# A two-layer hybrid attention trunk on one core: lanes are offered a turn once per row block outside the differential heads

## The chip, the cores and the metric

One core of a Trainium2 chip runs one program that computes both layers. The metric is the device time of one execution in microseconds (us). Every time below comes from such executions, or from one that a hardware profiler recorded.

## The reference

All is float32: 512 tokens of width 2048, 2 layers. Each layer normalises its input, projects it to 5952 columns, runs three groups of attention heads on slices of that, gates and concatenates them, projects back and adds a normalised residual:

```python
h = rms_norm(x, pre_w)
proj = h @ w_in                                   # 2048 x 5952
a_q, a_k, a_v, a_g, b_q, b_k, b_v, b_g, c_q, c_kv, c_kr, c_g = split(proj)
y_a = diff_attention(...)            # 4 heads, two softmaxes each, causal
y_b = sliding_window_attention(...)  # 16 query heads on 2 key heads, window 128, sinks
qc  = rms_norm(c_q, q_norm_w) @ w_uq
kvc = rms_norm(c_kv, kv_norm_w) @ w_ukv
y_c = causal_attention(...)          # 4 latent heads with a shared rotary key
y = concatenate([y_a, y_b, y_c]) * silu(concatenate([a_g, b_g, c_g]))
out = y @ w_out                                   # 2048 x 2048
return x + rms_norm(out, post_w)
```

## The kernel before

**Products in three parts.** A float32 product is made of three matmuls on a shorter format: both factors are split into a high and a low half, and high x high, high x low and low x high are summed in PSUM (`three`, line 299; each matmul is issued on line 142). The high half of a weight tile, `whi`, is a cast on ScalarE (L151), the low half, `wlo`, a subtraction of two SBUF tiles (L152) on VectorE or GpSimd. Before the line `ahead[0] = True` (L701) and from the second half of the output projection on, every other `wlo` is made on VectorE; in between all are made on GpSimd, ahead of other work.

**Row blocks.** The weights come in row blocks of 128 rows. `stream` loads two at a time on SP's queue into one of three buffers (`raw`) and yields their halves. `sweep` (L306) takes a block, or a group of two at the start and at the end of a projection, and for each bank of PSUM (a "job": one 128-token tile, or 128 columns of the result) issues its matmuls. A projection has 4 banks, or 2 where it covers half of the tokens, so a block is 12 (or 6) matmuls, and a group of two 24 (or 12). All four banks (`g`) come from one pool of four: the next projection's first bank must first have been read out by VectorE or ScalarE.

**Lanes.** The work on heads runs beside the projections as two "lanes". A lane is a Python generator whose steps issue a few TensorE instructions and the VectorE and ScalarE work that follows them, then yield a delay. `Lanes.step` runs a lane's next step only if the planner's clock, which `mm` and `transpose` advance by an assumed cost, has passed that delay (2.6 us for a split, 3.0 for a row of scores, more elsewhere, L1040 to L1053). `Lanes.tick` (L92) offers both lanes one step. `sweep` calls it after each job and after the group. `lanes.finish` forces named tasks to their end where the next part needs them. TensorE's order is the order in which Python issues it; the other engines' order is found by a scheduler.

**The order of a layer** (times of layer 0 in the profile; layer 1 repeats it):

- Feed (start; and the turn from one layer to the next): `feed` (L510) transposes 128-token tiles (`hT`), scales them (`h`) and splits them into `act_hi` and `act_lo`; at the turn `finish` (L968) first makes the residual, `ob` (L982), in whose rows the next layer's input lies. `scale` squares the same rows for the norm. Beside them run the keys' and the first queries' projections of each half of the tokens; `rotate_q` turns the queries on VectorE (L242 to L252: `q_rot`). `layer_constants` computes lambda with an Exp on ScalarE (`lam_d`, L494).
- 116 to 280 us: two gate projections, then the second queries' projection. `spread_r` makes the row scales, `sw_pair` (L652) runs two sliding-window heads: `stack_q` transposes four tiles of `q_rot` (`qT`) and splits them (`qe`, `qo`, L380 and L381), then scores (`sc`), probabilities (`p`), their transposes and split (`pT`, `pTh`, `pTl`), and the sum over values (`oT`).
- 280 to 490 us: the low-rank projections (`C_Q`, `C_KV`) with the other four pairs of heads; `latent_scale` with `rsqrt` (L160 to L165, `rsq_u`, `rlat`); the rotary queries (`qr`) and their stacks (`rotary_q`, L777); `up_kv` (L789), which needs these and the spread scale `R` before it can read out its banks (`kf`, `vl`); the gate of the latent heads, with two of them as lanes (`mla_head`).
- 498 to 725 us: the differential heads' four projections and their gate, with `da_head` as lanes.
- From 725 us: the output projection in four chunks of 512 columns, the last two in two halves of the tokens.

The loop that the change touches, and what calls it:

Of the kernel before, what the change touches and what calls it, by code (L numbers as in the profile page):

```python
# [108 lines left out]
def trunk(ctx: ExitStack, tc: tile.TileContext, ins, inv_freq, out):  # L109
# [164 lines left out]
            V.tensor_tensor(dst[:, mm_, :], src[:, mm_, :], rb, op=ALU.mult)  # L274


    ahead, behind = [False], [True]

    def stream(w, segs, nk, C, rows=0, before=None):

# [25 lines left out]
    def sweep(tiles, nk, jobs, after=None):  # L306

        def run(group):  # L310
            for job in jobs:
                for n, t in group:
                    job(t, n == 0, n == nk - 1)
                if job is not jobs[-1]:
                    lanes.tick()
            for n, t in group:
                if after:
                    after(n)
            lanes.tick()

        held = []
        for n, t in enumerate(tiles):
            held.append((n, t))
            if n in (0, nk - 2):
                continue
            run(held)
            held = []
# [219 lines left out]
    def norm_rows(name, l, tag):  # L547

        rows = []
        for n in range(4):  # L550
            rows.append(slot(name, tag))
            nc.gpsimd.dma_start(out=rows[n], in_=ins[name][l, n * S:(n + 1) * S].partition_broadcast(P))
        return rows

    def layer(l, pre, norms, r_in, start=None):
# [292 lines left out]
        for k in range(4, 12):  # L848
            gates[k] = slot("yb", "gy")
            nc.gpsimd.dma_start(out=gates[k], in_=y_spill[l][:, k - 4, :])  # L850
        stage = [0] * 5
        heads_out = [None] * 4

        def da_head(lane, h, raw, vv):
# [95 lines left out]
        done = [0]  # L950


        final = l + 1 == DEPTH
        post = norm_rows("post_norm_w", l, "k")
        nxt = None if final else column("pre_norm_w", l + 1, KT)
# [73 lines left out]
    for _ in range(N_LOAD):  # L1029
        load()  # L1030
    state = layer(0, pre, norms, r_in, start)
    for l in range(1, DEPTH):
        state = layer(l, *state)
# [41 lines left out]
```

## Time and profile before

| | |
|---|---|
| three executions | 1810.54, 1814.18 (median) and 1814.90 us |
| the profiled execution | 1823.35 us, of which the span of the trace is 1821.6 us |
| TensorE busy in the span | 1746.5 us (96%), 8832 matmuls |
| TensorE's mean granted clock | 0.986 of 2.4 GHz |
| VectorE, ScalarE, GpSimd busy | 914.7, 820.4 and 788.0 us (50, 45 and 43%) |
| DMA | 202.26 MB, 111 GB/s on the mean |

Busy time of TensorE is the union of its matmuls' times, so what is missing to the span is the time in which it waited. An instruction that waits blocks the ones behind it on its engine. A matmul of 512 columns is shown with some 0.40 us, but the next starts 0.23 us after it. The granted clock has two levels, 2.4 and 1.2 GHz; a share between is a mean over the stretch. TensorE, VectorE and ScalarE are told apart in rows as PE, DVE and ACT; POOL is GpSimd.

### The profile page before, as it was taken

What the parts mean: (1) busy time and instruction counts of PE and PEld (TensorE: products, weight loads), DVE (VectorE), ACT (ScalarE), POOL (GpSimd) and SP (SyncE); (2) the same over time, 40 slices, a digit from 0 to 9 for tenths busy, and PEclk for the clock granted to TensorE, in tenths of its full rate; (3) what the DMA queues carried; (4) which work ended last, traced back from release to release, by engine and by line L of the source; (5) the groups of instructions that cost most, each with busy time, mean ns of one, the idle gap of its engine ahead of it and who ended that gap; (6) DMA issues with size and microseconds to landing.
All of it is one profiled execution on the core that took longest, in us unless ns stands there. A gap on an engine that the chain in (4) does not pass through costs nothing. (4 is left out here: it accounts for less than half of the span.)

```text
span 1821.6 us, 25325 instructions
## 1 busy us (share of the span) xinstructions
PE 1746.5 (96%) x8832; PEld 1495.5 (82%) x8832; DVE 914.7 (50%) x2230; ACT 820.4 (45%) x1792; POOL 788.0 (43%) x666
## 2 busy tenths in 40 slices
PE   6899999999999999999979999999999999999996
PEld 5778888878899998788768788788889999888875
DVE  7754616734336658301785554275434357680033
ACT  6444524625344445325555553264444344552343
POOL 4343343343434344448334334334434434444662
PEclk9999999999999999999999999999999999999999
DMA  6542332232323233325755323322323322332366
GB/s 186 142 139 76 92 97 67 88 84 79 101 85 85 67 90 120 116 93 184 240 174 168 93 81 94 92 70 87 87 70 116 81 70 71 115 128 93 123 200 197
DMA packets 168672, 202.26 MB, mean 111 GB/s; under 512 B 30800, under 2 KB 92256, under 8 KB 168544
## 3 DMA queue, kind: packets, MB, share of 16 engines
q1 hardware_dynamic: 162160, 190.12, 35.3%
q0 software_dynamic: 3264, 10.51, 1.6%
q8 instruction: 69, 1.13, 0.3%
q10 hardware_dynamic: 3120, 0.01, 0.1%
q14 instruction: 59, 0.48, 0.1%
HBM read 188.02 MB, written 12.58 MB: 110 GB/s over the span
## 5 line engine op out<-in xcount | busy, mean ns | idle before, releaser
L152 POOL TENSOR_TENSOR wlo<-raw,whi 128x512 fp32r<-128x512 f32 (+2 forms) x608 | 758.2, 1254 | 987.9 <-ACT whi L151 955.3
L151 ACT CAST whi<-raw 128x512 fp32r<-128x512 f32 (+3 forms) x704 | 405.0, 582 | 602.8 <-PE g L142 487.7
L142 PE MATMUL g<-wlo,act_hi 128*128 128x512 f32 (+2 forms) x1408 | 523.5, 372 | 25.6 <-DVE wlo L152 23.8
L142 PE MATMUL g<-whi,act_hi 128*128 128x512 f32 (+2 forms) x1408 | 527.1, 374 | 7.2 <-ACT whi L151 7.2
L142 PE MATMUL g<-whi,act_lo 128*128 128x512 f32 (+2 forms) x1408 | 519.6, 369 | 0.0
L142 PEld LDWEIGHTS g<-wlo,act_hi 128*128 128x128 f32 x1408 | 267.9, 190 | 69.8 <-DVE wlo L152 31.7
L142 PE MATMUL g<-act_hi,whi 128*128 128x512 f32 x768 | 314.4, 409 | 0.0
L142 PE MATMUL g<-act_hi,wlo 128*128 128x512 f32 x768 | 305.9, 398 | 0.0
L142 PE MATMUL g<-act_lo,whi 128*128 128x512 f32 x768 | 305.7, 398 | 0.0
L142 PEld LDWEIGHTS g<-whi,act_hi 128*128 128x128 f32 x1408 | 268.0, 190 | 43.2 <-ACT whi L151 8.8
L142 PEld LDWEIGHTS g<-whi,act_lo 128*128 128x128 f32 x1408 | 267.8, 190 | 34.4
L142 PEld LDWEIGHTS g<-act_hi,wlo 128*128 128x128 f32 x768 | 145.6, 190 | 35.1
L142 PEld LDWEIGHTS g<-act_hi,whi 128*128 128x128 f32 x768 | 146.5, 191 | 28.6
L142 PEld LDWEIGHTS g<-act_lo,whi 128*128 128x128 f32 x768 | 146.3, 190 | 28.8
L152 DVE TENSOR_TENSOR wlo<-raw,whi 128x512 fp32r<-128x512 f32 (+1 forms) x96 | 71.3, 745 | 100.9 <-ACT whi L151 100.9
L966 DVE TENSOR_TENSOR ob<-g,post_norm_w 128x512 f32<-128x512 f32 x32 | 22.1, 691 | 192.0 <-ACT sq L964 191.9
L152 DVE TENSOR_TENSOR pTl<-pT,pTh 128x512 fp32r<-128x512 f32 (+2 forms) x112 | 67.8, 610 | 68.7 <-ACT pTh L151 68.5
L151 ACT CAST pTh<-pT 128x512 fp32r<-128x512 f32 (+2 forms) x112 | 58.6, 526 | 71.3 <-PE pT L146 70.7
L367 DVE TENSOR_TENSOR gate<-g,r_rows 128x512 f32<-128x512 f32 x32 | 22.0, 689 | 86.9 <-PE g L142 85.8
L146 PE MATMUL pT<-ident,p 128*128 128x128 f32 x384 | 61.0, 274 | 1.3 <-DVE p L833 1.3
L644 ACT ACTIVATE p<-p,nm 128x256 f32<-128x256 f32 (+1 forms) x128 | 59.8, 469 | 0.0
L438 ACT ACTIVATE p<-p,nm 128x128 f32<-128x128 f32 (+3 forms) x64 | 36.0, 562 | 49.8 <-DVE nm L437 49.8
(236 smaller groups left out, 2079.5 us busy)
## 6 DMA issues: line engine op xcount, KB each, us to landing
raw<-w_in SPq DMA_DIRECT2D x144, 512.0 KB, 3.7
raw<-w_out SPq DMA_DIRECT2D x96, 512.0 KB, 3.8
raw<-w_in SPq DMA_DIRECT2D x192, 128.0 KB, 2.4
raw<-w_in SPq DMA_DIRECT2D x32, 256.0 KB, 3.1
x<-x SPq DMA_DIRECT2D x16, 256.0 KB, 4.7
y_spill<-gate POOLq DMA_DIRECT2D x16, 256.0 KB, 2.3
raw<-w_ukv SPq DMA_DIRECT2D x8, 512.0 KB, 3.8
yb<-y_spill POOLq DMA_DIRECT2D x16, 256.0 KB, 4.1
```

The costliest lines, as they stand in the source:

```text
L142: nc.tensor.matmul(out_, a, b, start=start, stop=stop, skip_group_check=True)
L146: nc.tensor.transpose(out_, in_, ident)
L151: late(A.copy(hi, src), behind)
L152: E.tensor_tensor(lo, src, hi.bitcast(F32), op=ALU.subtract)
L367: V.tensor_tensor(gate, ps, rows, op=ALU.mult)
L438: A.activation(p, p, AF.Exp, bias=nm, scale=scale, accum_out=den)
L644: A.activation(blocks[i], blocks[i], AF.Exp, bias=nm[:, i:i + 1], scale=64.0 ** -0.5, accum_out=den[:, i:i + 1])
L966: V.tensor_tensor(ob[n][m], t, post[n], op=ALU.mult)
```

## The change

A switch, `fine`, is added. It is false at first, is set just before the differential heads' projections of a layer, and is cleared after their gate projection, ahead of the output projection. The turn after each job but the last is offered only while it is set. The turn after each group stays everywhere.

```diff
-    ahead, behind = [False], [True]
+    ahead, behind, fine = [False], [True], [False]
...
             for job in jobs:
                 for n, t in group:
                     job(t, n == 0, n == nk - 1)
-                if job is not jobs[-1]:
+                if fine[0] and job is not jobs[-1]:
                     lanes.tick()
...
         stage = [0] * 5
+        fine[0] = True
         heads_out = [None] * 4
...
         done = [0]
 
 
+        fine[0] = False
         final = l + 1 == DEPTH
```

On TensorE, at the start of layer 0's first gate projection, before (`g_1278` and `g_1279` are its first and second bank, `whi_1284` and `whi_1288` its first two row blocks):

```order
L142 MATMUL g_1278<-act_hi_88,whi_1284 128x512
L142 MATMUL g_1278<-act_lo_89,whi_1284 128x512
L142 MATMUL g_1278<-act_hi_88,wlo_1285 128x512
L142 MATMUL g_1278<-act_hi_88,whi_1288 128x512
L142 MATMUL g_1278<-act_lo_89,whi_1288 128x512
L142 MATMUL g_1278<-act_hi_88,wlo_1289 128x512
L146 MATMUL qT_1307<-ident_83,q_rot_850 128x128
L146 MATMUL qT_1307<-ident_83,q_rot_856 128x128
L146 MATMUL qT_1307<-ident_83,q_rot_1264 128x128
L146 MATMUL qT_1307<-ident_83,q_rot_1270 128x128
L142 MATMUL g_1279<-act_hi_88,whi_1284 128x512
```

and now, where `g_1281` is the fourth bank (the second and third, twelve matmuls, stand ahead of these rows):

```order
L142 MATMUL g_1281<-act_hi_88,whi_1284 128x512
L142 MATMUL g_1281<-act_lo_89,whi_1284 128x512
L142 MATMUL g_1281<-act_hi_88,wlo_1285 128x512
L142 MATMUL g_1281<-act_hi_88,whi_1288 128x512
L142 MATMUL g_1281<-act_lo_89,whi_1288 128x512
L142 MATMUL g_1281<-act_hi_88,wlo_1289 128x512
L146 MATMUL qT_1325<-ident_83,q_rot_850 128x128
L146 MATMUL qT_1325<-ident_83,q_rot_856 128x128
L146 MATMUL qT_1325<-ident_83,q_rot_1264 128x128
L146 MATMUL qT_1325<-ident_83,q_rot_1270 128x128
L142 MATMUL g_1278<-act_hi_88,whi_1338 128x512
```

The four transposes of the first query stack stood behind the first bank's six matmuls and stand now behind the fourth bank's, 18 matmuls later. The first stacks of the second four pairs, in the projection `C_Q`, move in the same way.

On VectorE, where layer 0's rotary queries are read out of PSUM (`qr<-g`, and with `rope` turned) while the scale of the latent keys is worked out (`ms`, `rsq_u`, `rlat`), before:

```order
L246 TENSOR_TENSOR qr<-g,cos 128x256
L739 TENSOR_TENSOR ms<-css,r_sq_1277 128x4
L252 TENSOR_TENSOR qr<-qr,rope 128x256
L740 TENSOR_SCALAR ms<-ms 128x4
L242 TENSOR_TENSOR rope<-g,sin 128x4x32
L160 TENSOR_SCALAR rsq_u<-ms 128x4
L244 TENSOR_TENSOR rope<-g,sin 128x4x32
L161 TENSOR_SCALAR rlat<-rsq_u 128x4
L246 TENSOR_TENSOR qr<-g,cos 128x256
L163 TENSOR_TENSOR rsq_u<-rlat 128x4
```

and now, from the third of the four tiles on:

```order
L246 TENSOR_TENSOR qr<-g,cos 128x256
L242 TENSOR_TENSOR rope<-g,sin 128x4x32
L252 TENSOR_TENSOR qr<-qr,rope 128x256
L244 TENSOR_TENSOR rope<-g,sin 128x4x32
L246 TENSOR_TENSOR qr<-g,cos 128x256
L252 TENSOR_TENSOR qr<-qr,rope 128x256
L739 TENSOR_TENSOR ms<-css,r_sq_1277 128x4
L740 TENSOR_SCALAR ms<-ms 128x4
L160 TENSOR_SCALAR rsq_u<-ms 128x4
```

The two chains alternated from the second tile on, and now the scale follows the last tile.

On ScalarE, at the turn to layer 1, in the first queries' projection, around the Exp of lambda (`lam_d`); `vb` and `kd` are the read-out of the projection ahead of it, before:

```order
L154 ACTIVATE vb<-g,r_in_8116 128x64
L151 CAST whi<-raw 128x512
L250 COPY kd<-kd 128x3x64
L154 ACTIVATE vb<-g,r_in_8116 128x64 x2
L250 COPY kd<-kd 128x3x64
L154 ACTIVATE vb<-g,r_in_8116 128x64
L151 CAST act_hi<-h 128x4x128
L494 ACTIVATE lam_d<-lam_d 128x2
L151 CAST whi<-raw 128x512 x6
```

and now:

```order
L154 ACTIVATE vb<-g,r_in_8116 128x64
L151 CAST whi<-raw 128x512
L250 COPY kd<-kd 128x3x64
L154 ACTIVATE vb<-g,r_in_8116 128x64
L151 CAST whi<-raw 128x512
L154 ACTIVATE vb<-g,r_in_8116 128x64
L250 COPY kd<-kd 128x3x64
L154 ACTIVATE vb<-g,r_in_8116 128x64
L151 CAST whi<-raw 128x512 x2
L151 CAST act_hi<-h 128x4x128
L494 ACTIVATE lam_d<-lam_d 128x2
L151 CAST whi<-raw 128x512 x6
```

Of this projection's weight casts three stood ahead of these rows and one in them, four in all ahead of the Exp; now it is two and four, six in all.

## Rows read from the trace of the kernel before

**Rows 1.** The page, part 1: busy us (share of the span) xinstructions.

```profile
PE 1746.5 (96%) x8832; PEld 1495.5 (82%) x8832; DVE 914.7 (50%) x2230; ACT 820.4 (45%) x1792; POOL 788.0 (43%) x666
```

**Rows 2.** Busy time by stretch, columns as the first line says.

```profile
core 0: us, PE busy (x) PEld busy (x) DVE busy (x) ACT busy (x) POOL busy (x), PEclk, DMA share, GB/s
0.00:60.00 60.00, 39.01 (x198) 33.86 (x199) 47.19 (x116) 35.83 (x85) 22.19 (x30) 0.91 0.60 169
...
116.00:124.00 8.00, 6.33 (x23) 4.72 (x22) 4.71 (x7) 1.68 (x3) 2.82 (x2) 0.79 0.46 133
...
160.00:260.00 100.00, 100.00 (x485) 82.70 (x484) 42.79 (x98) 41.88 (x93) 43.31 (x35) 1.00 0.30 90
280.00:288.00 8.00, 6.23 (x24) 4.81 (x23) 5.95 (x11) 2.60 (x5) 2.68 (x2) 0.79 0.23 67
...
498.00:725.00 227.00, 224.48 (x1271) 211.93 (x1270) 135.79 (x343) 106.86 (x236) 95.90 (x88) 0.99 0.33 93
...
916.00:960.00 44.00, 34.47 (x182) 29.69 (x181) 37.46 (x90) 23.51 (x57) 15.44 (x13) 0.92 0.61 184
...
1010.00:1018.00 8.00, 6.33 (x22) 4.75 (x21) 4.82 (x7) 1.78 (x3) 2.93 (x2) 0.79 0.45 131
1174.00:1183.00 9.00, 7.02 (x29) 5.51 (x28) 6.26 (x11) 2.79 (x5) 2.97 (x2) 0.81 0.19 58
...
...
1760.00:1800.00 40.00, 35.68 (x143) 27.34 (x142) 20.04 (x32) 15.33 (x28) 16.00 (x12) 0.96 0.79 250
```

**Rows 3.** TensorE's groups, shapes apart: busy us, mean ns | idle us before, releaser.

```profile
L142 PE MATMUL oT<-pTl,vb 128*128 128x256 f32 x96 | 25.9, 284 | 1.6 <-DVE pTl L152 1.6
L142 PE MATMUL g<-ch,whi 128*128 128x512 f32 x64 | 25.6, 400 | 2.5 <-DVE rsq_u L164 2.5
...
L146 PE MATMUL qT<-ident,q_rot 128*128 128x128 f32 x64 | 11.3, 292 | 7.1 <-DVE q_rot L252 7.1
...
L142 PE MATMUL sc<-kh,qe 128*128 128x128 f32 x28 | 6.9, 247 | 1.3 <-DVE qe L380 1.3
```

**Rows 4.** TensorE's waits: 0 to 110, 860 to 1000, 1740 to 1822 us; us, times, longest.

```profile
PE g L142 <- DVE wlo L152: 12.6, 9, 6.5
...
PE g L142 <- DVE wlo L152: 7.9, 9, 2.8
PE g L142 <- ACT whi L151: 3.6, 1, 3.6
PE hT L146 <- DVE ob L982: 2.6, 2, 1.8
...
PE g L142 <- DVE wlo L152: 3.3, 2, 3.0
```

**Rows 5.** Timeline of TensorE, 278 to 290 us: start, us, instruction [idle before, releaser].

```profile
279.41 0.40 PE L142 MATMUL g<-act_hi,whi 128*128 128x512 f32 x1
...
280.81 0.38 PE L146 MATMUL qT<-ident,q_rot 128*128 128x128 f32 x2
281.61 0.33 PE L146 MATMUL qT<-ident,q_rot 128*128 128x128 f32 x1 [0.42 <-DVE q_rot L252]
283.29 1.09 PE L146 MATMUL qT<-ident,q_rot 128*128 128x128 f32 x5 [1.35 <-DVE q_rot L252]
...
285.02 0.63 PE L142 MATMUL g<-act_hi,wlo 128*128 128x512 f32 x1
285.45 0.63 PE L142 MATMUL g<-act_hi,whi 128*128 128x512 f32 x1
```

**Rows 6.** Timeline of VectorE, 274 to 290 us.

```profile
281.81 0.68 DVE L246 TENSOR_TENSOR q_rot<-g,rcos 128x512 f32<-128x512 f32 x1
282.52 0.71 DVE L252 TENSOR_TENSOR q_rot<-q_rot,rope 128x512 f32<-128x512 f32 x1
```

**Rows 7.** VectorE, 1755 to 1790 us, and line 982 over the span.

```profile
1763.28 4.82 DVE L982 SCALAR_TENSOR_TENSOR ob<-ob,rout,xo 128x512 f32<-128x512 f32 x4
...
L982 DVE SCALAR_TENSOR_TENSOR ob<-ob,rout,xo x32: 735/747/1824, 868.9 to 1816.8; 128x512 f32<-128x512 f32 x32
```

## The prediction

> **What bounds the kernel now.** First read is the page's busy line: TensorE 1746.5 us of the span of 1821.6 us, VectorE 914.7 us [rows 1]. The program is a TensorE queue that almost never stands still, so an edit that adds and removes no TensorE work can win or lose only in the 75.1 us in which that engine is idle, and in the stretches in which it runs at the lower clock. The second view, busy time by stretch, says where these are [rows 2]. In steady projections there is none: 160 to 260 us holds 100.00 us busy of 100.00, with both lanes at work. The loss sits in the start (39.01 of 60 us, granted clock 0.91), the layer turn (34.47 of 44 us, 0.92), the end (1760 to 1800 us: 35.68 of 40 us, 0.96) and four short places of 8 or 9 us (at 116, 280, 1010 and 1174 us) with about 1.7 us idle and a mean clock of 0.79 to 0.81. The third view, TensorE's groups with shapes kept apart, gives the idle time ahead of each and its releaser: 7.1 us for q_rot, 2.5 for rsq_u, 1.6 for pTl, 1.3 for qe, over both layers [rows 3]. Start, turn and end, in the view of who waited for whom, wait for something else, mostly wlo, the low halves of the weights split on VectorE: 12.6, 7.9 and 3.3 us [rows 4].
>
> One such place, row by row: at 281.61 a transpose of q_rot has waited 0.42 us, at 283.29 the next 1.35 us, and the gate projection's matmuls, which need nothing of q_rot, stand behind them [rows 5]. Then TensorE is at 1.2 GHz: matmuls start at 285.02 and 285.45, 0.43 us apart, where the six from 279.41 to 280.81 started 1.40 / 6 = 0.233 us apart, at 2.4 GHz.
>
> **The change, part by part.** Counts stay: the order has 8224 TensorE rows in both kernels, and no matmul, split or transfer is added. Outside the stretch from the first differential projection to the end of their gate projection a lane is now offered a turn once per row block (12 matmuls of 512 columns, or 24 for the two-block groups at either end), no longer after each bank's 3 or 6. At 0.233 us each a turn comes every 2.8 or 5.6 us instead of every 0.7 or 1.4.
>
> *q_rot, four places.* The first stack of queries moves from behind the first bank of the gate (or low-rank) projection to behind its fourth: 18 matmuls later, 18 x 0.233 = 4.2 us. VectorE's last q_rot starts at 282.52 and takes 0.71 us, so it is done at 283.2 [rows 6]; the transposes would come at 280.81 + 4.2 = 285.0. The wait goes, with 1.8 us to spare, and so do its three likes: 7.1 us. What is late next is the fourth bank, which the same VectorE chain empties: its last read (q_rot<-g) ends at 281.81 + 0.68 = 282.5 and its matmuls would start at 279.41 + 18 x 0.233 = 283.6: 1.1 us to spare, a nearer miss than the transposes. With the wait goes the low clock behind it, since in 160 to 260 us the same lanes' transposes, without a wait, run at 1.00 [rows 2]: 3 x 8 x 0.21 + 9 x 0.19 = 6.8 us. Together 13.9; if the clock falls all the same, 7.1; if the bank takes the wait over, 0.
>
> *Lane waits for qe and pTl.* A lane's score and probability steps now stand a whole row block behind what they read, where they stood as near as its delay of 2.6 us allowed. Of 1.6 + 1.3 [rows 3] I take all: 2.9 us, between 0 and 2.9, since two lanes that turn at the same place also ask VectorE at the same time; 160 to 260 us, where before already turns both lanes together, shows that this need not cost anything.
>
> *rsq_u.* In the order the reciprocal-root chain of the key-value scale is no longer woven into the rotation of the rotary queries but stands behind it, so the bank that the next projection waits for is emptied first. 2.5 us in both layers; nothing hides it now, and at worst it stays: 0. The scale itself is late by a block or two, which the 72 matmuls of up_kv cover.
>
> *Layer turn.* The first transposes of the residual (hT behind ob, 2.6 us in two waits [rows 4]) come 9 and 6 matmuls later (2.1 us, and 0.9 at the 0.147 us of 320 columns), worth 1.8. The wait of 3.6 us for whi is ScalarE's queue: the casts stand behind the Exp of lambda, which waits for its constants. Six casts instead of four now stand ahead of it; two row blocks of 6 matmuls are 2.8 us of cover, of which I take 2.0, as VectorE's own queue there is filled too. The 7.9 us for wlo I leave: the order only reshuffles them. Sum 3.8. The ends are everything there (14.1 of waits and 0.08 x 44 = 3.5 of clock) and 4 us lost, half of the wlo waits again.
>
> *Start.* VectorE is busy 47.19 of 60 us [rows 2] and carries rotary tables, activations and every other weight split. In the order its third weight split moves from row 30 to row 11, so about 12 matmuls can run inside the longest wait; at 0.15 to 0.27 us that is 1.8 to 3.2 us. VectorE's total work sets the end of this stage, so I take 2.0; between 5 lost (the next wait grows by as much) and 6.5 gained (that wait gone).
>
> *End.* The residual's DMA stores are moved on SP's queue by some loads, but on VectorE one weight split still stands behind four residual adds, which take 4.82 us [rows 7]. I take 0 of the 3.3 us, between 3 lost and 5 gained (with the clock's 0.04 x 40 = 1.6).
>
> The same line's median is 0.747 us and its longest 1.824 [rows 7], so four of them should take 3.0. The Trainium skill (SBUF — State Buffer, section Who interferes with whom) says that a VectorE instruction with two SBUF inputs and a GpSimd instruction that reads SBUF exclude each other, and the second waits until the first is done; both the adds and GpSimd's weight splits are of that kind. By it 1.8 us of this wait is a matter of how the two fall together, and the term would lie anywhere from -1.8 to +1.8; by the unchanged order it is 0. It speaks against turns in larger groups, as more adds then meet the splits. The trace agrees as far as the spread goes.
>
> *What the change adds.* The second stack of rotary queries no longer fits in under up_kv's matmuls and is forced behind them. Queued behind its four transposes is the output gate's projection of the latent heads; its fourth bank is emptied by a value split that now stands behind two more VectorE operations (0.69 us each, as in rows 6). 1.4 us less the slack there, twice: I take 0.5 lost, between 0 and 2.8. The lanes' own transfers (spilled heads on POOL's queue, residual loads and stores on SP's) come some us later and are read a stage or a layer later.
>
> Sum: 13.9 + 2.9 + 2.5 + 3.8 + 2.0 + 0 - 0.5 = 24.6 us. The profiled execution took 1823.35 us, of which 1.75 lie outside the span: 1823.35 - 24.6 = 1798.8. The median shown, 1814.18, is 0.9950 of the profiled execution; 1798.8 x 0.9950 = 1790.
>
> **The rivals.** *Half of it* (0.18): the q_rot and rsq_u waits go, but the clock falls all the same, and the lane waits return as bursts on VectorE. 7.1 + 2.5 = 9.6 us: 1805 at the median. For it: VectorE is the releaser everywhere. Against: 160 to 260 us.
>
> *The turn and the start clear up too* (0.15): all of 17.6 us in place of 3.8, and 6.5 in place of 2.0: 42.9 us, 1771. For it: both are pile-ups of lane work ahead of weight splits, and turns are now further apart. Against: VectorE has 37.46 of 44 us of work there whatever the order.
>
> *The wait moves to the bank* (0.08): the fourth bank is late by what the transposes were; 13.9 us stay, other gains and losses cancel, and the time is within 5 us of before. For it: only 1.1 us of slack, from the same chain.
>
> *Slower* (0.07): weight splits that VectorE does stand behind whole groups of lane work, as at 1763 us, and TensorE starves at start, turn and end. Were those waits to double, 12.6 + 7.9 + 3.3 = 23.8 us and their clock, 5.4 + 3.5 + 1.6 = 10.5, are added: 34.3 lost against 19.3 won in the middle, 15 us slower, 1829 at the median. It decides once the waits grow by more than 19.3 / 34.3, a little over half. Against: the order gives these splits an earlier place at the start, and about the same at turn and end.
>
> That the steps don't move at all is excluded by the order, so no chance is kept for it.
>
> **How the numbers follow.** My forecast has 0.52; its own range is 1780 to 1799. Changes below 0.3% (5 us) can't be told from none here. Faster by more: 0.52 + 0.18 + 0.15 = 0.85, of which I move 0.02 to no change, since the half case ends near that line: 0.83. Within 0.3%: 0.10. Slower: 0.07. The range that should hold 8 of 10 takes in the forecast, the half case and the near side of the larger one: 1776 to 1807.
>
> **What would show it.** In the waits of TensorE, q_rot, rsq_u, qe and pTl in the sliding-window and low-rank stages are gone or below 1 us, and the granted clock at the four places is 1.00. At the turn, whi's 3.6 us is near 1, while wlo is still the largest entry, with some 20 us in all. The stretch of layer 0's differential heads stays as it is, 224.48 us busy of 227 [rows 2]. I am wrong if TensorE waits for a bank read by L246, if the clock stays low without a wait, or if the waits for wlo pass 35 us.

## The result, and the profile after

The changed kernel took 1792.14 us in the median, the kernel before 1814.54 us beside it: a ratio of 0.9877 (95% interval 0.9857 to 0.9897). A second comparison, with other executions of both, gave 0.9866 (0.9848 to 0.9884). That is 22 to 24 us less, where 24.6 were forecast against the profiled execution and 1790 us as the time. The profiled execution of the changed kernel took 1790.03 us, of which its span is 1788.2.

The page's busy line of the changed kernel (columns as in [rows 1]):

```profile
PE 1731.7 (97%) x8832; PEld 1488.4 (83%) x8832; DVE 911.0 (51%) x2230; ACT 820.4 (46%) x1792; POOL 787.1 (44%) x666
```

TensorE now idles for 56.5 us of the span instead of 75.1. The work is the same, so the 15 us less of busy time must be low clock that is gone and modelled ends of matmuls that no longer stand ahead of a wait; how much is which was not measured.

Busy time of the changed kernel by stretch, columns as in [rows 2]: the start, then three of the four q_rot places, then the differential heads of layer 0, the turn and the end:

```profile
0.00:60.00 60.00, 42.67 (x210) 37.03 (x211) 48.28 (x123) 38.00 (x88) 24.11 (x31) 0.91 0.63 178
114.00:122.00 8.00, 8.00 (x38) 6.52 (x37) 4.25 (x6) 2.56 (x5) 5.03 (x4) 1.00 0.42 130
271.00:279.00 8.00, 8.00 (x40) 6.56 (x40) 4.33 (x9) 3.71 (x8) 5.60 (x4) 1.00 0.22 66
484.00:711.00 227.00, 224.47 (x1272) 211.88 (x1271) 135.72 (x343) 106.86 (x237) 95.74 (x88) 0.99 0.33 94
903.00:947.00 44.00, 37.00 (x191) 30.36 (x190) 38.32 (x89) 25.16 (x57) 15.82 (x13) 0.96 0.64 191
1151.00:1160.00 9.00, 9.00 (x46) 7.43 (x45) 5.28 (x10) 4.18 (x8) 5.27 (x4) 1.00 0.25 65
1727.00:1767.00 40.00, 36.93 (x153) 29.06 (x152) 21.05 (x36) 16.51 (x29) 17.15 (x13) 0.96 0.80 256
```

At the q_rot places TensorE never stops, and the granted clock is 1.00 where it was 0.79 to 0.81. The start, turn and end still hold most of the idle time. The groups of TensorE that waited in [rows 3], in the changed kernel:

```profile
L142 PE MATMUL oT<-pTl,vb 128*128 128x256 f32 x96 | 25.7, 282 | 0.0
L142 PE MATMUL g<-ch,whi 128*128 128x512 f32 x64 | 25.7, 401 | 0.0
L146 PE MATMUL qT<-ident,q_rot 128*128 128x128 f32 x64 | 8.9, 272 | 0.0
L142 PE MATMUL sc<-kh,qe 128*128 128x128 f32 x28 | 6.6, 236 | 0.0
```

All four are at zero. TensorE's waits at start, turn and end (0 to 108, 843 to 983 and 1707 to 1788 us, against [rows 4]):

```profile
PE g L142 <- DVE wlo L152: 13.1, 6, 5.6
...
PE g L142 <- DVE wlo L152: 10.6, 8, 2.7
...
PE hT L146 <- DVE ob L984: 0.5, 1, 0.5
...
PE g L142 <- DVE wlo L152: 3.1, 1, 3.1
```

The wait for ScalarE's cast behind the Exp (3.6 us) is gone and the one for the residual is down from 2.6 to 0.5, but the wait for wlo at the turn has grown from 7.9 to 10.6. The place of [rows 5] in the changed kernel (it lies in the projection `C_Q`, not in a gate projection as the prediction has it), TensorE's timeline from layer 0's first `C_Q` matmul (start, us, instruction):

```profile
270.83 0.40 PE L142 MATMUL g<-act_hi,whi 128*128 128x512 f32 x1
...
275.04 0.40 PE L142 MATMUL g<-act_hi,whi 128*128 128x512 f32 x1
...
276.43 1.04 PE L146 MATMUL qT<-ident,q_rot 128*128 128x128 f32 x8
277.23 0.48 PE L142 MATMUL g<-act_hi,whi 128*128 128x512 f32 x1
277.54 0.39 PE L142 MATMUL g<-act_lo,whi 128*128 128x512 f32 x1
```

and VectorE's last two operations on q_rot there:

```profile
273.23 0.68 DVE L246 TENSOR_TENSOR q_rot<-g,rcos 128x512 f32<-128x512 f32 x1
...
273.95 0.73 DVE L252 TENSOR_TENSOR q_rot<-q_rot,rope 128x512 f32<-128x512 f32 x1
```

The fourth bank is read out at 273.91 and first written at 275.04: 1.1 us to spare, as computed. The transposes come at 276.43, 1.75 us behind q_rot's end. All eight transposes, two stacks, stand in one turn, as they did here in [rows 5].

**By stage.** Each row below is the time between the starts of the same two TensorE matmuls in both traces, before less after, beside the forecast's terms for that stretch. The row of the first output chunks takes in, for layer 1, the first half of the last two chunks too.

| stretch (layer 0, layer 1) | before | after | gained | forecast |
|---|---|---|---|---|
| start, to the first gate projection | 115.65 | 113.29 | 2.4 | 2.0 |
| gate projections to `C_Q` | 163.8, 163.8 | 157.5, 157.6 | 6.2, 6.2 | 4.9, 4.9 |
| `C_Q` to the differential heads | 218.5, 218.7 | 213.1, 213.1 | 5.3, 5.6 | 4.5, 4.5 |
| differential heads | 227.4, 227.4 | 227.4, 225.8 | 0.0, 1.6 | 0 |
| first output chunks | 92.3, 137.1 | 91.3, 136.1 | 1.0, 1.0 | 0 |
| rest of layer 0's output, and the turn | 192.2 | 190.2 | 2.0 | 3.8 |
| end | 51.5 | 49.5 | 2.0 | 0 |

These two executions are 33.3 us apart, 11 us more than the medians of the first comparison (22.4). Where the 11 us are from was the first question.

### The profile page after: what moved, and what is told of

It is laid out like the page before. It is cut to its first block, busy times and chain, and to the rows that moved or that the text cites. A ratio compares the mean times of both kernels' runs of the same rounds, so it can differ in the third digit from the quotient of the medians.

```text
span 1788.2 us, 25330 instructions
## 1 busy us (share of the span) xinstructions
PE 1731.7 (97%) x8832; PEld 1488.4 (83%) x8832; DVE 911.0 (51%) x2230; ACT 820.4 (46%) x1792; POOL 787.1 (44%) x666
## 5 line engine op out<-in xcount | busy, mean ns | idle before, releaser
L142 PE MATMUL g<-wlo,act_hi 128*128 128x512 f32 (+2 forms) x1408 | 522.5, 371 | 28.8 <-DVE wlo L152 26.8
L152 DVE TENSOR_TENSOR wlo<-raw,whi 128x512 fp32r<-128x512 f32 (+1 forms) x96 | 67.0, 701 | 97.7 <-ACT whi L151 97.6
L436 DVE CUSTOM_DVE_ANT_0 p<-sc,causal 128x128 f32<-128x128 f32 (+3 forms) x96 | 46.1, 480 | 33.0 <-PE sc L142 33.0
L438 ACT ACTIVATE p<-p,nm 128x128 f32<-128x128 f32 (+3 forms) x64 | 36.0, 562 | 51.5 <-DVE nm L437 51.4
```

Source lines behind the costliest of these rows:

```text
L142: nc.tensor.matmul(out_, a, b, start=start, stop=stop, skip_group_check=True)
L152: E.tensor_tensor(lo, src, hi.bitcast(F32), op=ALU.subtract)
L436: V.tensor_tensor_reduce(p, scores, mask, 1.0, -3e38, op0=ALU.add, op1=ALU.max, accum_out=mx)
L438: A.activation(p, p, AF.Exp, bias=nm, scale=scale, accum_out=den)
```

## The experiments

**The kernel before once more.** No edit.

> The kernel before, unchanged, for a second trace of it. Its first trace (1823.35 us) is 8.8 us above the median of its unprofiled executions (1814.54), so a sum made against that trace may hold something that other executions lack. Theory A (the waits and the lower clock belong to the program): ratio 1.000, and the second trace shows the same waits (q_rot 7.1 us, wlo 23.8) and the same granted clock, 0.79 to 0.81 at the four q_rot places, 0.95 in the differential heads of both layers. Rival B (the wait belongs to the program, the fall of the clock behind it comes in some executions and not in others): ratio 1.000, the same waits, but at some of these places a clock of 1.00, and a time lower by 1.6 to 1.8 us for each.

Measured: 0.9994 (0.9976 to 1.0013). Busy time by stretch of this second trace, at the first gate projection, at `C_Q` of layer 0, and over the differential heads of both layers:

```profile
116.00:124.00 8.00, 6.35 (x32) 4.93 (x31) 5.15 (x9) 2.50 (x5) 2.97 (x2) 1.00 0.46 133
279.00:287.00 8.00, 6.23 (x24) 4.72 (x23) 5.78 (x10) 2.45 (x5) 2.51 (x2) 0.79 0.24 67
494.00:722.00 228.00, 225.49 (x1294) 212.96 (x1293) 137.95 (x346) 108.44 (x240) 97.66 (x90) 1.00 0.33 95
1388.00:1616.00 228.00, 225.48 (x1294) 212.97 (x1293) 137.85 (x346) 108.48 (x240) 97.78 (x90) 1.00 0.32 96
```

Rival B holds. The waits are nearly the same (q_rot 7.1 us again, wlo 24.0 instead of 23.8, no entry off by more than 0.5), but at 116 us the clock is 1.00 behind the same idle 1.65 us where it was 0.79 in [rows 2], and both differential stages take 225.8 us instead of 227.4. A fall of the clock costs 1.6 us (62.64 against 61.08 us for the same first gate projection; 227.4 against 225.8 for a differential stage). Over all traces of this study in which the stage's code is the same, it came at the `C_Q` place in 6 of 6 passages, at the first gate in 3 of 6, and behind the 1.7 us wait in the differential heads in 9 of 22. The unprofiled executions show it too: of 57 of the kernel before, the 13 with a mean clock of 0.991 or more took 1813.8 us on the mean, the 20 with 0.987 or less 1820.4. The first trace of before had all six falls that these places can have, where by these counts some four are usual; the changed kernel's had one. So the first trace of before holds some 3 to 5 us more of low clock than the usual one (2 falls) or the second one (3 falls). The rest of the 11 us lies in the start, the turn and the end, which differ from trace to trace, and was not followed up.

**The four places alone.** In the kernel before, the turns between banks are left out only in the first group of the first gate projection and of `C_Q`:

```diff
+            quiet, once[0] = once[0], False
             for job in jobs:
...
-                if job is not jobs[-1]:
+                if not quiet and job is not jobs[-1]:
...
+        once[0] = True
         gate_chunk(B_G, 4)
...
+        once[0] = True
         ps = gemm_T(act, w_in, [(C_Q, S)])
```

> The kernel before with one part of the change: only in the first group of the first gate projection and of C_Q, in both layers, are the turns between banks left out (four places in all). Forecast's terms: the q_rot waits and the low clock behind them go, 13.9 us, ratio 0.992, about 1800.6 us, and the waits for qe, pTl and rsq_u (5.4 us) stay. By the two traces these stretches could hold more: 116 to 279 us gained 6.2 and 279 to 397 us 4.7 us in layer 0, of which 1.8 were qe and pTl; so up to 18 us, ratio 0.990. Rival (half of it): the wait goes and the clock falls all the same, 7.1 us, 0.996.

Measured: 0.9969 (0.9954 to 0.9984), 5.6 us. By stage, `C_Q` to the low-rank products gained 4.1 and 4.3 us, as expected, but the gate stage lost 1.5 us in layer 0 and gained 1.7 in layer 1. TensorE's waits in the gate stage of layer 0, 110 to 280 us:

```profile
PE oT L142 <- DVE pTl L152: 2.0, 1, 2.0
PE sc L142 <- DVE qe L381: 1.8, 1, 1.8
```

The wait for q_rot (1.7 us) is gone and two others have grown by 2.3 together (they were 0.8 and 0.7). Behind each the clock fell: 0.79 on the mean from 131 to 139 and from 148 to 156 us. In layer 1 only the one for qe is there (1.8 us, and one fall). VectorE's timeline shows why:

```profile
130.04 0.85 DVE L647 TENSOR_TENSOR den<-den,es 128x4 f32<-128x4 f32 x1 [3.21 <-ACT p L645]
...
131.21 1.07 DVE L650 TENSOR_SCALAR p<-p,den 128x128 f32<-128x128 f32 x4
132.31 0.68 DVE L381 TENSOR_TENSOR qe<-qT,qe 64x512 fp32r<-64x512 f32 x1
```

The second lane's stack was transposed at 126.21 and its qe was split at 132.31, behind the first lane's softmax. With turns back between banks, the second lane's scores were asked for at 131.3, too early again.

**The middle alone, and the ends alone.** Both are edits of the changed kernel. In the first, `fine` starts true and is cleared for the middle:

```diff
-    ahead, behind, fine = [False], [True], [False]
+    ahead, behind, fine = [False], [True], [True]
...
         ahead[0] = True
+        fine[0] = False
...
-        fine[0] = False
         final = l + 1 == DEPTH
```

> The changed kernel with turns between banks kept in the feed, the turn of the layers and the output projection, so that only the stretch from the gate projections to the latent heads has one turn per row block. Forecast's terms: 13.9 + 2.9 + 2.5 - 0.5 = 18.8 us, ratio 0.9896. From the two traces: 6.2 + 4.7 + 0.7 and 6.2 + 4.9 + 0.7 = 23.4 us, 0.987. If the executions of before at the median had fewer falls of the clock than the profiled one, less: 0.991.

The converse:

```diff
         ahead[0] = True
+        fine[0] = True
```

> The converse: one turn per row block only in the feed, the turn of the layers and the output projection; the stretch from the gate projections to the latent heads as before. Forecast's terms: start 2.0, turn 3.8, end 0: 5.8 us, ratio 0.9968. From the two traces: start 2.4, turn 2.0, first chunk of the output projection 1.0 twice, end 2.0: 8.4 us, 0.9954. Rival (the slower case: weight splits behind whole groups of lane work): above 1.000. The two parts are expected to add up to the whole, 0.9877.

Measured: the middle 0.9884 (0.9857 to 0.991), 21 us; the ends 0.9982 (0.9966 to 0.9997), 3.3 us. Together 24.4, and the whole took off 22 to 24. So most of the gain is the middle's. The intervals are wide (16 to 26 us for the middle, 0.5 to 6 for the ends): neither the forecast's 18.8 for the middle nor its 5.8 for the ends is excluded by these timings.

**Distance or grouping?** In the kernel before, turns stay between banks, and only the sliding-window lanes' delays are made longer:

```diff
+            if pr < 2:
+                yield 4.5
             qq = stack_q(lane, f"qE{lane}", qt[g], 128 * pr)
-            yield L_SPLIT
+            yield 2 * L_SPLIT
```

(and so at the two other delays of 2.6 us in `sw_pair`).

> The kernel before, with turns between banks everywhere, but with longer delays in the sliding-window lanes: 4.5 us ahead of the first two stacks of each half, and 5.2 in place of 2.6 us between a stack or a transposed block and what reads it. Theory D (what counts is the distance between a lane's step and what it reads, however the turns are grouped): the waits for q_rot, qe and pTl go as in the changed kernel, 4.6 to 6.2 us in the gate stages and 4.7 in the low-rank ones, twice: 18.6 to 21.8 us against the first trace, ratio about 0.990; rsq_u's 2.5 us and the ends stay. Rival G (steps have to come in groups, once per row block): the wait moves on to the next step as it did with the four places alone, under 6 us, 0.997 or above.

Measured: 0.9915 (0.9892 to 0.9938), 15.5 us. TensorE's waits from 110 to 275 us, and from 270 to 410:

```profile
PE oT L142 <- DVE pTl L152: 1.0, 1, 1.0
...
PE g L142 <- DVE cl L155: 1.6, 2, 1.2
PE g L142 <- DVE rsq_u L164: 0.8, 1, 0.8
```

Theory D: without any grouping the gate stage gained 5.0 us in each layer (6.2 in the changed kernel) and `C_Q` to the low-rank products 4.7 and 4.9, as much as in the changed kernel. What stays is rsq_u and a new wait for `cl`, as the lanes now end later: the two projections of the low-rank queries, 20.6 us before, take 23.3 and 22.2. The whole falls short of the 18.6 us expected, and is far from rival G's 6. The four places alone failed at the gate because only the first step was moved away from what it reads.

**One turn more at the four places.** The changed kernel, with a turn behind the second bank there too:

```diff
-                if fine[0] and job is not jobs[-1]:
+                if (fine[0] and job is not jobs[-1]) or (two and job is jobs[1]):
```

> The changed kernel with one more turn at the four q_rot places, behind the second bank: the first stack then stands 6 matmuls (1.4 us) later than before the change and 12 earlier than after it. Of the wait of 0.42 + 1.35 us some 0.4 us should be left at each place. If the clock falls only behind the longer waits (1.7 us and more), the cost is 4 x 0.4 = 1.6 us against the changed kernel, ratio to before 0.9886; if it falls behind this wait too, 4 x 2.0 = 8 us, 0.992. The next step, which reads qe, is offered a whole row block later as in the changed kernel, so qe should not be waited for.

Measured: 0.9891 (0.9871 to 0.991); over the whole span q_rot was waited for 2.3 us in all:

```profile
PE g L142 <- DVE cl L155: 5.7, 8, 0.9
...
PE qT L146 <- DVE q_rot L252: 2.3, 4, 0.6
```

Busy time by stretch at the two places of layer 0:

```profile
114.00:124.00 10.00, 9.49 (x47) 7.70 (x46) 6.18 (x16) 4.35 (x10) 5.29 (x4) 1.00 0.38 108
271.00:281.00 10.00, 9.38 (x54) 7.83 (x53) 8.22 (x19) 4.81 (x8) 4.90 (x4) 1.00 0.22 70
```

The clock is 1.00, in layer 1 too: behind waits of 0.5 to 0.6 us it did not fall. These are what 6 matmuls leave of the old wait (0.4 was expected), and the gate stage took only 0.7 us more than in the changed kernel. But a new wait came, for the banks that `cl` is split from, as the lanes' work stands nearer to it: `C_Q` to the low-rank products took 4.1 us more in each layer. So the ratio agrees with the expectation of 0.9886, but not for its reason: the traces are 8 to 11 us apart and the medians (1800.2 and 1792.1 us) 8, while the ratios say 2.5, as the kernel before took longer in this comparison (1819.9 us in the median).

**The exception taken away.** The changed kernel without `fine[0] = True`: one turn per row block in the differential heads' stage too.

> The changed kernel without its exception: one turn per row block in the differential heads' stage too. Theory: these heads have the longest chain of steps (a turn per row block is 12 x 0.175 = 2.1 us there, so delays of 2.6 and 3.0 us are rounded up to 4.2), their lanes fall behind and are forced at the end of a projection, where the waits stand open: slower than the changed kernel, by 5 to 20 us, ratio to before 0.990 to 0.999. Rival: as elsewhere, the waits of that stage (oT behind pTl 1.7 us in each layer, and the low clock behind it, 1.6 us where it falls) go: 3.4 to 6.6 us faster than the changed kernel, 0.984 to 0.986.

Measured: 1.0018 (1.0004 to 1.0033): about 26 us slower than the changed kernel, more than expected. TensorE's waits over the span:

```profile
PE R L142 <- DVE dh L458: 14.4, 4, 6.8
PE pT L146 <- DVE p L894: 6.8, 6, 2.3
...
PE g L142 <- DVE gate L367: 4.2, 2, 2.1
```

In layer 0 the stage lost 5.2 us and the first output chunks 6.9 against the changed kernel, in layer 1 8.6 and 6.9. The longest wait lies inside the stage, ahead of the fourth head's projection, and comes again in layer 1:

```profile
617.75 0.77 PE L142 MATMUL R<-dh,ones_r 128*128 128x512 f32 x1 [6.76 <-DVE dh L458]
```

There the program forces the first head to its end, and the head's last chain (`css`, `rsub`, `dh`, `R`) is run with no matmuls of a projection behind it: lanes forced at the end of a projection, as the theory had it. Of the 6.9 us in the output chunks 3.2 are waits. The rest is TensorE work of the last heads that has moved there from the stage: 32 of the heads' instructions instead of 13, 5.3 us instead of 1.6. The 3.4 us wait of oT for pTl did go, as the rival had it.

**What is left.** Edits of the changed kernel at the waits that remain: the weight splits of VectorE, and oT behind pTl. First, three of four low halves on GpSimd:

```diff
-                    split(hi, lo, raw[:, i, 0:C], behind=behind[0], E=nc.gpsimd if ahead[0] or i else V)
+                    split(hi, lo, raw[:, i, 0:C], behind=behind[0], E=nc.gpsimd if ahead[0] or i or k0 % 4 else V)
```

> The changed kernel with three of four low halves of the weights on GpSimd, no longer two of four, in the start, the turn and the end (48 splits leave VectorE). TensorE still waits 26.8 us for wlo of VectorE there. If VectorE's queue is the cause, the wait falls to about half: 10 to 13 us faster than the changed kernel, ratio to before 0.981. Rival: GpSimd takes 1.25 us for a split of 512 columns where VectorE takes 0.70, and a block of 6 matmuls lasts 1.4 us at 512 and 0.88 us at 320 columns, so the wait turns from VectorE to GpSimd's wlo: no gain, or some us slower, 0.987 to 0.992.

Measured: 0.9865 (0.9842 to 0.9889), the same as the changed kernel within the intervals; the wait for VectorE's wlo went from 26.8 to 23.8 us only. With `turned[0]`, true from the first gate projection on, in place of `k0 % 4`:

> The changed kernel with all low halves of the weights on GpSimd from the first gate projection on, at the turn of the layers and at the end too; the start as in the changed kernel. With three of four on GpSimd the turn's weights still waited for VectorE (a single wait of 3.4 us, behind a residual product and a rotary table). Theory: GpSimd's 1.25 us a split keep up with a block of 6 matmuls of 512 columns (1.4 us), so VectorE's part of the waits from 840 us on, 10.6 us at the turn and some 3.2 at the end, goes for the larger part: 6 to 10 us faster than the changed kernel, 0.982 to 0.984. Rival: at 320 columns a block lasts 0.88 us and GpSimd is the bound: no gain, 0.987 or above.

Measured: 0.9937 (0.9922 to 0.9951), 13 us slower than the changed kernel. Its waits:

```profile
PE g L142 <- ACT whi L151: 17.0, 5, 7.2
PE g L142 <- DVE wlo L152: 13.1, 8, 5.5
PE hT L146 <- DVE ob L984: 5.2, 4, 2.6
```

VectorE's wlo waits are left at the start alone (13.1), yet whi, `ob` and `h` are waited for instead. That GpSimd holds up the whole chain of weight buffers is likely, but no run separates it. With a longer delay ahead of one sum over values, `4.6 if h < 2 else L_SPLIT`:

> The changed kernel with a longer delay (4.6 in place of 2.6 us) at one step of the first two differential heads of a layer: between the second block of transposed probabilities and the sum over values that reads its low half. Theory D (distance): the wait of oT for pTl, 1.7 us in each layer, goes, and with it the fall of the clock that came behind it in 8 of 18 passages, 1.6 us each: 3.4 + 1.4 = 4.8 us faster than the changed kernel, 0.9851. Rival: VectorE's queue there is full (the wait stands behind the rotation of the next head), and the wait moves to the next head's transposes (qT or kT): no gain, 0.987 to 0.988.

The changed kernel itself, beside these:

> The changed kernel once more, timed beside the three that follow, to measure them against it and not only against the kernel before. Ratio to before 0.9877 as in the first comparison (0.9857 to 0.9897). Theory B (falls of the clock come in some executions): its executions lie closer together than those of before, since fewer waits are left for the clock to fall behind.

And all low halves on GpSimd together with the longer delay:

> The changed kernel with both of these edits. They touch different stages, so the gains should add: 0.980 to 0.982 by the theories, no better than the changed kernel by the rivals.

Measured: 0.9862 (0.9846 to 0.9877) for the longer gap against 0.9866 (0.9848 to 0.9884) for the changed kernel beside it. The wait for pTl is gone, and two of 0.9 us for the next head's `p` have come:

```profile
PE pT L146 <- DVE p L895: 1.8, 2, 0.9
```

So a gain of 0.5 us a layer is left of the 1.7, and the rival (the wait moves on) holds for the rest. Both edits together: 0.9921 (0.9906 to 0.9936), what GpSimd loses less some 3 us. Theory B's closer executions did not show: the changed kernel's four span 5.1 us here, nine of the kernel before 7.4, with a standard deviation of 2.4 and 2.3 us. No version was measurably faster than the changed kernel.

## Why the prediction was right

- **The bound** (TensorE's queue, idle in few places): right. The gain lies mostly where the prediction put it, 21 of 22 to 24 us in the middle.
- **q_rot, four places, 13.9 us:** the waits and the low clock went, with the slack computed at the bank. But the argument from the position of one stack alone does not carry the whole term: that edit by itself brought 5.6 us. At `C_Q` it worked, at the gate the next step is late instead. The changed kernel moves all steps of a lane, and so does the version with longer delays. The low clock was also counted at all four places; at the first gate it falls in about half of the passages.
- **qe and pTl, 2.9 us:** they went, and gave more. The gate stage gained 4.7 us a layer without any fall of the clock in the trace of before (162.2 to 157.5). The idle column misses part of a wait, as the matmul ahead is shown busy for 0.17 us after its successor could have started: by starts, the four waits there are 0.48 + 1.56 + 0.82 + 0.98 = 3.8 us, and the idle column has 3.2. Where the remaining 0.9 us are from is open. Fewer changes between the lanes' and the projection's matmuls (44 instead of 52 in this stage) can be little of it: the version with longer delays has 56, and without its one wait of 1.0 us its stage takes 157.8 us.
- **rsq_u 2.5, forced stack -0.5:** net 1.4 instead of 2.0 over both layers. From the low-rank queries' products to the last of the first key-value products each layer gained 1.7 us, and from there to the differential heads it lost 1.0, where 0.25 were forecast; a wait of 0.3 us for the value split (L155 `vl`) is part of it.
- **Turn, 3.8 us:** mis-sized. The two waits named (hT, whi) went as said, 2.1 and 3.6 us, but wlo took 2.7 back. Over six traces with turns per row block and five with turns between banks, the stretch takes 191.4 and 192.4 us on the mean (190.2 to 193.0 and 191.8 to 193.6): 1.0, and not clear of the spread. In the whole program wlo is waited for 26.8 us, where the prediction expected some 20.
- **Start, 2.0 us:** the pair of traces says 2.4, but eight traces with the new order at the start reach the first gate projection at 113.3 to 116.0 us (114.5 on the mean), five with the old at 113.5 to 116.0 (115.0). That is 0.5 on the mean, far inside the spread: a gain at the start is not shown.
- **End, 0:** 1.5 us over the same traces (51.0 to 49.5). VectorE's four residual adds did not change at all: 4.82 us again, and the wait behind them is 3.1 us. What went stands behind it: by starts, 1.0 us of wait for a weight load and 0.9 us in two waits for wlo.
- **Not foreseen:** the first output chunk gained 1.0 us in each layer, as the last head's step that reads `dh` is offered a row block later; TensorE waited for it before (R behind dh, 0.45 us in each layer) and no longer does.
- **Why the sum still came out:** in part by luck. By the traces, terms that were too large (the turn, the start, the low clock at the gate) stand against terms that were too small (qe and pTl, the end, the output chunks). And the sum was taken from the profiled execution of before, from which the changed kernel's is 33.3 us away and not 24.6; scaling it to the median by 0.9950 made up for this, for a reason that the prediction did not know: that execution stood 9 us above the median, in part because the clock had fallen at more places in it.

On the rule of the Trainium skill (SBUF — State Buffer, section Who interferes with whom): the four adds took 4.82 us in the changed kernel too, and the spread of the line is the same (734, 746 and 1830 ns least, median and most, where [rows 7] have 735, 747 and 1824). The trace agrees with the rule add by add. The first and the fourth of the four started 0.01 and 0.11 us behind a weight split on GpSimd and took 1.83 and 1.74 us, the two between them 0.74. The first of them, GpSimd's row ahead of VectorE's:

```profile
1732.00 1.29 POOL L152 TENSOR_TENSOR wlo<-raw,whi 128x512 fp32r<-128x512 f32 x1 [1.50 <-ACT whi L151]
...
1732.01 1.83 DVE L984 SCALAR_TENSOR_TENSOR ob<-ob,rout,xo 128x512 f32<-128x512 f32 x1
```

It was the same in the kernel before (0.02 and 0.09 us behind, 1.82 and 1.74 us), so the time is the same because the two engines meet in the same way. Over the whole line, 5 of 32 adds before and 6 of 32 after start within a split on GpSimd. Each of these 11 ends 0.55 us after the split does and so takes 0.8 to 1.8 us; all others take 0.73 to 0.75. Nothing here shows that turns in larger groups make VectorE's adds meet GpSimd's splits more often.

## What to carry to other kernels

Where a queue that must not stop has work of other chains woven in, what counts is how far each step stands behind what it reads, by the real time of the engine in between, and this for all steps of a chain: moving one of them can hand the wait to the next, as at the gate. Longer distances cost little while the chain has time left, and a great deal where it hasn't: the same edit was worth 21 us beside the sliding-window and latent heads and -26 us beside the differential heads. Before a stage is costed from one trace, a second trace of the same kernel shows which of its parts come and go.

## What was not expected of the hardware

The granted clock after a wait is not a property of the program. Behind idle times of 1.35 to 1.7 us in one piece it fell to the lower level in some passages and not in others (6 of 6, 3 of 6, 9 of 22 at three places), and a fall cost 1.6 us; behind waits of 0.5 to 0.6 us it stayed at 1.00 at all four places. That a kernel without such waits is also steadier is not shown: the changed kernel's eight executions lie between 1790.0 and 1796.1 us, the 57 of before between 1809.8 and 1823.2, but so few lie closer together in any case, and within one comparison the spread was the same.
